# Router's 1/rms taken ahead of the last token rows, the first expert's tokens split ahead of the slot table, and the feed-forward block's first weights loaded and split ahead of the last down product

## The chip, the core and the metric

The program runs on one core of a Trainium2 chip. The metric is the device time of one execution in microseconds (us). The core has a matrix engine (PE, with its weight loads shown apart as PEld), a vector engine (DVE), a scalar engine (ACT), GpSimd (POOL) and the sync engine (SP), which issues most of the loads. Each engine runs its own list of instructions in order. An instruction that waits for a semaphore holds up everything behind it in that list, and 16 DMA engines move the data.

## The reference

Two transformer blocks stand one behind the other, over 512 tokens of 1024 features, in float32. The first ends in a mixture of experts (MoE), the second begins with a feed-forward block (FFN). Cut to what the change touches:

```python
# end of the first block: h = rms_norm(x, norm_ffn_g), then two of 32 experts for each token
g_sel = argmax(h @ w_rg + b_rg)                     # one of 4 groups
top_v, top_i = top_k(expert logits of that group, 2)
e_w = softmax(top_v) * g_w
x = x + sum over the two experts of
        e_w * ((silu(h @ w_gate[e]) * (h @ w_up[e])) @ w_down[e])
x = rms_norm(x, norm_final_g)
# second block
x = x + 0.5 * ((silu(n @ w1_gate) * (n @ w1_up)) @ w1_down)   # n = rmsnorm(x, g_ffn1), 2816 wide
...                                                 # attention, then a second FFN
```

Every token's weight for an expert and the list of the tokens of each expert hang on the router's result, so they are known only at run time.

## The kernel before

The activations x lie in SBUF with features on the partitions, as 8 blocks of 128 features by 512 tokens. A float32 product is made of three passes on PE (`mm3`, lines 257 to 259). Both operands are split first into a rounded part and its remainder (`hilo`, lines 203 and 204): a cast on ACT gives `wh` (or the first half of a `t8`), and a subtraction on DVE gives `wl` (or its second half). Weights come in 1 MB tiles (`t8`, loaded on SP at line 238). Each tile gives two or four pairs of `wh` and `wl`, from a pool `wp` of three buffers each, so a fourth split waits until PE has done with the first pair.

**The router.** While the last projection of the mixer runs, each finished block k of x is squared and added to `hsq` (L215 on ACT, L217 on DVE), multiplied with the router's weights (L573), scaled (L576), transposed to rows (L579) and copied (L581). The rows are written to DRAM as `hrow` (L673). Then 1/rms is made from `hsq`: eight small products with ones on PE (L286), `var` (L315), a square root on ACT (L268) and a few small DVE operations give `rtok` (L273). From the logits DVE finds both experts of each token. Experts are ranked by their number of tokens. Two fixed experts come first; they have tables of their own (`tabf`), and their tokens are gathered by POOL with an indirect DMA from `hrow` (L1042). For the other 30 DVE works out a slot for each token and choice (L785 to L795; `dest`, cast to integers at L794). POOL scatters the pairs to a table in DRAM in eight indirect DMAs (L804) and loads it back as `tabb` for large experts and `tab2` and `tab3` for small ones (L824, L827, L832). The gathers of the third and later units read from these.

**The experts.** The units stand in a fixed order (`SEQ`): two fixed experts, a pair of small ones, a large one, and so on. The loop in `moe` takes turns: `up` of unit n+1 is issued ahead of `down` of unit n, and the features of unit n+2 (`expert_x`, L1052, or `small_x`, L954) between them. So PE transposes the gathered tokens of unit 2 right behind `up` of unit 1 and ahead of `down` of unit 0. `expert_x` splits the tokens with `hilo`. Weight loads go up to 13 tiles ahead (`MOE_WINDOW`); an expert's number is loaded to SP's registers first (L634). Large experts split their weights with two splits ahead of use (`SPLITS`). Small ones use the loaded tile as it is.

**The end of the MoE.** The last unit's up product (L972) is followed by its down product (L1005, scaled by L1011 and L1012). `spill` then holds a loop for experts with more tokens than a table holds (L896). Its body runs zero times with these inputs, but each engine goes through its branches and a barrier there. Behind it the last unit's result is added to x, block by block (L1024 on PE, L1025 on DVE), and each block is split for the FFN (L208 on ACT, L209 on DVE), whose first product is `w1_gate`'s.

The order on each engine is chosen by a scheduler when the kernel is built, from the program order and the dependences. Instructions given to `keep_in_program_order` are not moved against what stands around them. The functions below call these.

Of the kernel before, what the change touches and what calls it, by code (L numbers as in the profile page):

```python
# [117 lines left out]
class Net:  # L118
    def __init__(self, tc, ctx, A, out):
        self.tc, self.nc, self.A, self.out, self.ctx = tc, tc.nc, A, out, ctx  # L120
        nc = self.nc
        ec = ctx.enter_context
        self.own = None
        self.const = ec(tc.tile_pool(name="const", bufs=1))
        self.p8 = ec(tc.tile_pool(name="p8", bufs=16))
        self.p4 = ec(tc.tile_pool(name="p4", bufs=4))
        self.p2 = ec(tc.tile_pool(name="p2", bufs=5))
        self.wp = ec(tc.tile_pool(name="wp", bufs=3))
        self.sm = ec(tc.tile_pool(name="sm", bufs=2))
        self.pp = ec(tc.tile_pool(name="pp", bufs=8, space=PSUM))  # L130
        self.dr = ec(tc.tile_pool(name="dr", bufs=1, space=DRAM))
        c = self.const
        self.x = c.tile([128, ND, T], F32, name="x")
        self.vec = c.tile([128, NV], F32, name="vec")
        nc.scalar.dma_start(self.vec, A["vec"])
        self.cc = c.tile([128, NC_], F32, name="cc")
        nc.scalar.dma_start(self.cc, A["cc"])
        self.ident = self.cc[:, C_ID:C_ID + 128]
        self.ones = c.tile([128, 128], F32, name="ones")
        nc.vector.memset(self.ones, 1.0)  # L140
        self.table = self.dr.tile([ROUNDS * 128 * NE, 4], I32, name="table")
        self.ordd = self.dr.tile([1, NE], I32, name="ordd")
        self.hrow = self.dr.tile([T, D], F32, name="hrow")
        self.pay = c.tile([128, NT, 2, 4], I32, name="pay")
        self.br = c.tile([128, NG + NE], F32, name="br")
        self.order = c.tile([128, NE], I32, name="order")
        self.payf = c.tile([128, NT, NFIXED, 4], F32, name="payf")
        self.payi = c.tile([128, NT, 2], F32R, name="payi")
        self.g12 = c.tile([128, ND], F32, name="g12")
        o1, o2 = VOFF["norm_final_g"], VOFF["g_ffn1_2"]  # L150
        nc.vector.tensor_tensor(self.g12, self.vec[:, o1:o1 + ND], self.vec[:, o2:o2 + ND], op=ALU.mult)
# [48 lines left out]

    def hilo(self, hi, lo, src):
        nc = self.nc
        nc.scalar.copy(hi, src)  # L203
        nc.vector.tensor_tensor(lo, src, hi.bitcast(F32), op=ALU.subtract)  # L204

    def half(self, hi, lo, src, g):

# [346 lines left out]
    def router(self):  # L554
# [14 lines left out]

        def step(k):  # L570
            self.square(acc, self.x[:, k, :], k == 0)
            for i in range(NT):
                nc.tensor.matmul(lg[:, i * W:i * W + W], self.x[:, k, i * 128:i * 128 + 128], wr[:, k, :],  # L573
                                 start=k == 0 and i == 0, stop=k == ND - 1, skip_group_check=True)
# [53 lines left out]
    def mload(self, n):  # L628
        while self.wat < min(n, len(self.wkeys)):
            nm, p, h = self.wkeys[self.wat]  # L630
            if p not in self.wreg:
                e = p
                if p >= NFIXED:
# [1 line left out]
                self.wreg[p] = self.moe_weights(e)  # L635
            self.wraw[nm, p, h] = self.load8(self.wreg[p]["gud".index(nm)][h])()
            self.wat += 1

    def raw_next(self, key):

# [20 lines left out]
    def moe(self):  # L661
# [5 lines left out]
        ur, er = two[:, 0:128], two[:, 128:256]  # L667
        nc.gpsimd.tensor_copy(ur, self.cc[:, C_U:C_U + 128])
        nc.gpsimd.tensor_copy(er, self.ones)
        rt = self.rstd([self.hsq], D, "rtok")  # L670
        hrow, table, pay, payf = self.hrow, self.table, self.pay, self.payf
        for i in range(NT):
            nc.scalar.dma_start(hrow[i * 128:i * 128 + 128, :], rows[i])  # L673
# [101 lines left out]
        nc.vector.tensor_tensor(pf[0], o1[:, :, fx], bc(ds, NFIXED), op=mul)  # L775
        nc.vector.tensor_tensor(pf[0], pf[0], pf[1], op=add)
        nc.vector.tensor_copy(pf[1], rt.rearrange("p (i o) -> p i o", o=1).to_broadcast([128, NT, NFIXED]))
        for e in range(NFIXED):
            fixed2(e)
        P = small("P", NE)  # L780
        rowr, row, tmp = P, Em, P

        def all4(t):
            return t.rearrange("p (o e) -> p o e", o=1).to_broadcast([128, NT, NE])
        nc.vector.tensor_tensor(rowr, rk3, all4(less), op=add)  # L785
        nc.vector.scalar_tensor_tensor(rowr, rowr, 127.5, all4(less), op0=ALU.is_ge, op1=mul)
        nc.vector.tensor_tensor(rowr, rowr, rk3, op=add)
        nc.vector.scalar_tensor_tensor(row, rowr, float(NE), all4(rank), op0=mul, op1=add)
# [53 lines left out]
            else:  # L842
                self.gather(self.xts[n % 2][0:CAP], tabs[p][0:CAP])

        def features(n):
            xt = self.xts[n % 2]
            return self.expert_x(xt) if SEQ[n][0] < NBIG else self.small_x(xt)

        def up(n, xT, ys=()):
            unit = SEQ[n]  # L850
            tab = tabs[unit[0]]
# [12 lines left out]
        def down(n, aT):  # L864
# [3 lines left out]
            y = self.expert_down(self.split_next, aT, tab) if unit[0] < NBIG else self.small_down(unit, aT, tab)  # L868
            self.presplit(self.wnext + SPLITS)
            return [(t, sel) for t in y]  # L870
        a, ys = up(0, features(0)), ()
        xT = features(1)
        for n in range(NU - 2):
            aT = turn(n, a)
# [4 lines left out]
        aT, before = turn(NU - 2, a), ys  # L879
        ys = down(NU - 2, aT)  # L880
        a = up(NU - 1, xT, before)
        self.fst = self.ffn_stream(A["w1_gate"], A["w1_up"], A["w1_down"])
        for key in self.down_keys(SEQ[-1]):
            self.raw_next(key)
        self.add_small(ys)
        aT = turn(NU - 1, a)
        self.fst.load(FFN_FIRST)
        self.last = down(NU - 1, aT)
        self.fst.split(1)
        self.spill(rounds, trow)  # L890

    def spill(self, rounds, trow):
# [3 lines left out]
        with tc.For_i(1, nr, 1) as b:  # L896
            with tc.For_i(0, NE, 1) as p:
                A, B, C = (self.t8([128, 2048], dt) for dt in (F32R, F32, F32))
                P, Q = self.t2(), self.t2()
                G = self.t4([128, 1024], F32R)  # L900
                U, V = ([self.wp.tile([128, 2, 512], F32R, name=nm, tag=nm) for nm in ("wh", "wl")] for _ in range(2))
                X, Z = self.ps(), self.ps()
                self.own = {"t8": [A, B, C, B, C, B, C], "t4": [G, A[:, 0:D], A[:, D:2 * D]], "t2": [P, Q, G[:, 0:512]],
                            "w": [U, V] * 6, "ps": [X, Z, X, Z, X, X, Z] + [X, Z] * 4}
# [804 lines left out]
```

## Time and profile before

| what | value |
|---|---|
| time, median of 3 runs | 2027.65 us (2027.0 to 2028.92) |
| the profiled execution's own time | 2028.41 us |
| its span (first to last instruction) | 2026.5 us, so 1.9 us lie around it |
| busy share of the span | PE 95%, DVE 64%, ACT 35%, POOL 2% |
| mean granted clock of PE | 0.978 of full speed |
| read from memory | 339 MB, 170 GB/s over the span |

Times in the rows are microseconds from the start of the span. PE's busy share hides that the stretch from about 545 to 945 us, most of the MoE, has its DMA engines busy all the time, which the other stages don't.

### The profile page before, as it was taken

To read this page: it belongs to the slowest core of one execution; us is meant where nothing else is said; L and a number is where in the kernel's file an instruction comes from. 1 tells how busy PE (TensorE), PEld (TensorE's weight loads), DVE (VectorE), ACT (ScalarE), POOL (GpSimd) and SP (SyncE) were. 2 spreads that over 40 slices of the span, in tenths; PEclk is the share of its full clock that TensorE was granted. 3 is DMA by queue.
4 is the path that set the end of the run, shared out by engine and by line. 5 is a ranking of instruction groups with operands and counts; after the bars stand their busy time and mean duration, and the time that the engine had idled before them with its cause. 6 is when DMAs were issued, how large, how long until landed. Compare 5 with 4: busy or idle time off the path is not lost.

```text
span 2026.5 us, 24440 instructions
## 1 busy us (share of the span) xinstructions
PE 1918.1 (95%) x9375; PEld 1428.8 (71%) x9375; DVE 1293.8 (64%) x2234; ACT 715.6 (35%) x1116; POOL 48.4 (2%) x69
## 2 busy tenths in 40 slices
PE   7999999979998899887999999999989999999997
PEld 5898888867554353332788888887867788888886
DVE  7999997457777575555754442459999755444323
ACT  5334325345343221111532322336366633223221
POOL 0000001003000000000000000000000000000000
PEclk9999999988999999999999999999999999999998
DMA  6121232527999999998232224130111122222311
GB/s 258 53 87 60 104 124 104 236 108 271 385 409 409 408 416 408 410 420 334 85 104 94 94 79 170 66 151 1 53 50 47 48 83 92 96 94 83 151 57 42
DMA packets 60087, 341.59 MB, mean 169 GB/s; under 512 B 8208, under 2 KB 9168, under 8 KB 27456
## 3 DMA queue, kind: packets, MB, share of 16 engines
q1 hardware_dynamic: 55152, 329.87, 42.2%
q0 software_dynamic: 3520, 6.35, 1.0%
q10 hardware_dynamic: 1296, 3.79, 0.5%
q8 instruction: 74, 1.21, 0.2%
q14 instruction: 45, 0.37, 0.1%
HBM read 339.37 MB, written 4.54 MB: 170 GB/s over the span
## 4 chain that ended last, share of the span: by engine, by line
PE 47%; DVE 3%; ACT 2%; issue 0%; DMA 0%; DVEq 0%; ACTq 0%; SPq 0%
PE ps L257 15%; PE ps L259 14%; PE ps L258 14%; PE ps L1550 1%; ACT t L1524 1%; PE ps L1537 1%; DVE wl L204 0%; DVE t L204 0%; PE ps L1292 0%; ACT wh L203 0%; PE ps L1555 0%; DVE t L1520 0%; ACT t L203 0%; PE ps L295 0%; PE ps L1293 0%
## 5 line engine op out<-in xcount | busy, mean ns | idle before, releaser
L257 PE MATMUL ps<-t,wl 128*128 128x512 f32 x1728 | 684.2, 397 | 18.7 <-ACT t L208 18.3
L258 PE MATMUL ps<-t,wh 128*128 128x512 f32 x1728 | 681.2, 394 | 0.9 <-DVE t L209 0.9
L259 PE MATMUL ps<-t,wh 128*128 128x512 f32 x1728 | 681.4, 394 | 0.0
L203 ACT CAST wh<-t 128x1024 fp32r<-128x1024 f32 (+3 forms) x321 | 324.9, 1017 | 716.9 <-PE ps L259 532.7
L204 DVE TENSOR_TENSOR wl<-t,wh 128x1024 fp32r<-128x1024 f32 (+3 forms) x321 | 378.3, 1183 | 212.0 <-ACT wh L203 208.8
L257 PEld LDWEIGHTS ps<-t,wl 128*128 128x128 f32 x1728 | 325.3, 188 | 96.9 <-ACT t L208 19.1
L258 PEld LDWEIGHTS ps<-t,wh 128*128 128x128 f32 x1728 | 326.0, 189 | 76.8 <-DVE t L209 2.3
L259 PEld LDWEIGHTS ps<-t,wh 128*128 128x128 f32 x1728 | 325.3, 188 | 75.4
L257 PE MATMUL ps<-wh,t 128*128 128x256 f32 (+2 forms) x440 | 147.4, 337 | 23.2 <-DVE t L204 23.2
L972 PE MATMUL ps<-t,t 128*32 128x512 f32 (+1 forms) x832 | 162.6, 606 | 5.5 <-DMA t<-in_w_up 3.6
L403 DVE SCALAR_TENSOR_TENSOR t<-t,vec,t 128x512 f32<-128x512 f32 x240 | 165.7, 745 | 0.4
L1025 DVE TENSOR_TENSOR x<-x,ps 128x512 f32<-128x512 f32 x200 | 126.4, 683 | 44.9 <-PE ps L1024 44.1
L258 PE MATMUL ps<-wl,t 128*128 128x256 f32 (+2 forms) x440 | 145.7, 331 | 0.0
L259 PE MATMUL ps<-wh,t 128*128 128x256 f32 (+2 forms) x440 | 144.4, 328 | 0.0
L257 PEld LDWEIGHTS ps<-wh,t 128*128 128x128 f32 x440 | 85.8, 195 | 33.0 <-DVE t L204 25.1
L972 PEld LDWEIGHTS ps<-t,t 128*32 128x32 f32 (+1 forms) x832 | 41.4, 123 | 91.7 <-issue 78.8
L1181 DVE TENSOR_TENSOR t<-ps,rbc 128x512 f32<-128x512 f32 x44 | 30.4, 690 | 115.6 <-PE ps L259 115.6
L259 PEld LDWEIGHTS ps<-wh,t 128*128 128x128 f32 x440 | 85.9, 195 | 7.4
L258 PEld LDWEIGHTS ps<-wl,t 128*128 128x128 f32 x440 | 86.0, 195 | 6.8
L1024 PEld LDWEIGHTS ps<-t,t 128*128 128x128 f32 x248 | 42.8, 190 | 67.1 <-issue 31.6
L1024 PE MATMUL ps<-t,t 128*128 128x512 f32 x248 | 78.7, 424 | 11.5 <-DVE t L1012 7.4
L203 ACT CAST t<-t 128x512 fp32r<-128x512 f32 (+2 forms) x102 | 62.7, 619 | 57.5 <-DVE t L1182 26.2
(317 smaller groups left out, 1597.1 us busy)
## 6 DMA issues: line engine op xcount, KB each, us to landing
t<-in_w_down SPq DMA_DIRECT2D x80, 1024.0 KB, 19.8
t<-in_w_gate SPq DMA_DIRECT2D x64, 1024.0 KB
t<-in_w_up SPq DMA_DIRECT2D x64, 1024.0 KB, 19.2
t<-in_w_in SPq DMA_DIRECT2D x24, 1024.0 KB, 4.7
t<-in_w_gate SPq DMA_DIRECT2D x44, 512.0 KB
t<-in_w_up SPq DMA_DIRECT2D x44, 512.0 KB, 3.4
t<-in_w_down SPq DMA_DIRECT2D x8, 768.0 KB, 11.4
t<-in_w_qi SPq DMA_DIRECT2D x4, 1040.0 KB, 4.7
```

The source lines that it names most:

```text
L203: nc.scalar.copy(hi, src)
L204: nc.vector.tensor_tensor(lo, src, hi.bitcast(F32), op=ALU.subtract)
L257: mm(acc, a[1], b[0], start=first, stop=False)
L258: mm(acc, a[0], b[1], start=False, stop=False)
L259: mm(acc, a[0], b[0], start=False, stop=last)
L403: nc.vector.scalar_tensor_tensor(y[c], src, w, y[c], op0=mul, op1=add)
L972: nc.tensor.matmul(p[o:o + c, :], xT[:, k * CAP + i:k * CAP + i + c], w[:, q, :], start=k == 0, stop=k == ND - 1)
L1024: self.nc.tensor.matmul(p, yT[:, k * 128:k * 128 + 128], sel, start=j == 0, stop=j == n - 1)
L1025: self.nc.vector.tensor_tensor(self.x[:, k, :], self.x[:, k, :], p, op=ALU.add)
L1181: nc.vector.tensor_tensor(a, accs[1], rbc, op=mul)
L1524: nc.scalar.activation(part(i), part(i), AF.Exp, bias=nm[:, i:i + 1], scale=scale, accum_out=su[:, i:i + 1])
L1537: nc.tensor.transpose(tb[b][:, o + (i - s) * 128:o + (i - s) * 128 + 128], P[:, self.PO[i] + s * 128:self.PO[i] + s * 128 + 128], self.ident)
```

## The change

Four things are done.

1. The 1/rms (`rstd`) is built in the router's last step, ahead of the last block's transposes and of the writes of `hrow`.
2. In `moe`, the first weight splits and the features of unit 0 are issued ahead of the slot table. `keep_in_program_order` holds the splits and the first operation of the slot table (`rowr`) in their places.
3. At the end of the MoE the first two pieces of the FFN's weights (`w1_gate` and `w1_up`, 0.5 MB each) are loaded into one `t8` tile by a new `ffn_first`, called just ahead of the last unit's four down loads, and are split (`self.fst.split(FFN_FIRST)`, with `FFN_FIRST = 2`) ahead of its down product. Before, they were loaded behind the down loads, and one was split behind the down product, the other behind the loop.
4. The loop body in `spill` takes two of its working tiles from `t8` in place of `wp`. It is not executed with these inputs.

```diff
     def hilo(self, hi, lo, src):
         nc = self.nc
-        nc.scalar.copy(hi, src)
-        nc.vector.tensor_tensor(lo, src, hi.bitcast(F32), op=ALU.subtract)
+        pin = self.pin or (lambda ins: ins)
+        pin(nc.scalar.copy(hi, src))
+        pin(nc.vector.tensor_tensor(lo, src, hi.bitcast(F32), op=ALU.subtract))
...
             self.square(acc, self.x[:, k, :], k == 0)
+            if k == ND - 1:
+                self.rt = self.rstd([acc], D, "rtok")
             for i in range(NT):
...
             nm, p, h = self.wkeys[self.wat]
+            if (nm, p, h) == ("d", SEQ[-1][0], 0):
+                self.ffn_first()
...
+    def ffn_first(self):
+
+        A = self.A
+        self.fst = self.ffn_stream(A["w1_gate"], A["w1_up"], A["w1_down"])
+        t = self.t8([128, FFN_FIRST, ND, 128])
+        for i in range(FFN_FIRST):
+            self.nc.sync.dma_start(t[:, i], A[("w1_gate", "w1_up")[i % 2]][i // 2])
+            self.fst.raw[self.fst.items[i][0]] = t[:, i]
+        self.fst.load(FFN_FIRST)
...
-        rt = self.rstd([self.hsq], D, "rtok")
+        rt = self.rt
...
+        self.pin = tc.keep_in_program_order
+        self.presplit(SPLITS)
+        self.pin = None
         for e in range(NFIXED):
             fixed2(e)
+
+        def features(n):
+            xt = self.xts[n % 2]
+            return self.expert_x(xt) if SEQ[n][0] < NBIG else self.small_x(xt)
+
+        xT = features(0)
...
-        nc.vector.tensor_tensor(rowr, rk3, all4(less), op=add)
+        tc.keep_in_program_order(
+            nc.vector.tensor_tensor(rowr, rk3, all4(less), op=add))
...
-        a, ys = up(0, features(0)), ()
+        a, ys = up(0, xT), ()
...
         a = up(NU - 1, xT, before)
-        self.fst = self.ffn_stream(A["w1_gate"], A["w1_up"], A["w1_down"])
         for key in self.down_keys(SEQ[-1]):
             self.raw_next(key)
+        self.fst.split(FFN_FIRST)
         self.add_small(ys)
         aT = turn(NU - 1, a)
-        self.fst.load(FFN_FIRST)
         self.last = down(NU - 1, aT)
-        self.fst.split(1)
         self.spill(rounds, trow)
...
-                U, V = ([self.wp.tile([128, 2, 512], F32R, name=nm, tag=nm) for nm in ("wh", "wl")] for _ in range(2))
+                U, V = ([w[:, j] for j in range(2)] for w in (self.t8([128, 2, 2, 512], F32R) for _ in range(2)))
```

In the changed kernel the same statements have higher line numbers (`hilo` L205 and L206, `dest` L820, the scatters L830, the gathers L1062, `wl` and `t8` as before).

**DVE, the slot table and the first splits.** Before, the list reads as follows from the last reductions of the slot table on. `t8_3626` is the first expert's tokens, and `wl_3669` the fourth weight split; the first three stand further up, between the mixer's last blocks.

```order
L693 TENSOR_REDUCE rr0_3565<-t2_3444 128x4
L815 TENSOR_REDUCE cm_3600<-ce_3601 128x1
L794 CAST dest_3563<-rr0_3565 128x4
L792 TENSOR_TENSOR t2_3444<-t2_3444 128x128
...
L204 TENSOR_TENSOR t8_3626<-ps_3627,t8_3626 128x512
L794 CAST dest_3563<-rr1_3569 128x4
L818 TENSOR_SCALAR cm_3600<-cm_3600 128x1
L204 TENSOR_TENSOR t8_3626<-ps_3634,t8_3626 128x512
...
L204 TENSOR_TENSOR wl_3669<-t8_3011,wh_3668 128x1024
L204 TENSOR_TENSOR wl_3685<-t8_3013,wh_3684 128x1024
```

In the changed kernel the same stretch reads as follows; `wl_3663` is the third split, and the tokens are `t8_3567`.

```order
L206 TENSOR_TENSOR wl_3663<-t8_3009,wh_3662 128x1024
L206 TENSOR_TENSOR t8_3567<-ps_3568,t8_3567 128x512
L206 TENSOR_TENSOR t8_3567<-ps_3575,t8_3567 128x512
L811 TENSOR_TENSOR t2_3444<-ps_3481,less_3528 128x128
...
L709 TENSOR_REDUCE rr0_3588<-t2_3444 128x4
L841 TENSOR_REDUCE cm_3623<-ce_3624 128x1
L206 TENSOR_TENSOR wl_3669<-t8_3011,wh_3668 128x1024
L820 CAST dest_3586<-rr0_3588 128x4
...
L206 TENSOR_TENSOR wl_3685<-t8_3013,wh_3684 128x1024
L820 CAST dest_3586<-rr1_3592 128x4
```

The tokens' split moved ahead of the slot table. The fourth and the fifth weight split moved ahead of the first and the second cast to `dest`.

**POOL, the gathers of units 2 and 3.** Before, behind the table's loads, the gather of unit 2 (a pair of small experts, by `tab3`) stands ahead of that of unit 3 (a large one, by `tabb`).

```order
L832 DMA tab3_3620<-table_85 32x56
L832 DMA tab3_3620<-table_85 32x52
L832 DMA tab3_3620<-table_85 32x56
L832 DMA tab3_3620<-table_85 32x52
L1042 DMA t8_2990<-hrow_87,tab3_3620 64x1024
L1042 DMA t8_2990<-hrow_87,tabb_3615 128x1024
```

In the changed kernel:

```order
L858 DMA tab3_3643<-table_85 32x56
L858 DMA tab3_3643<-table_85 32x52
L858 DMA tab3_3643<-table_85 32x56
L858 DMA tab3_3643<-table_85 32x52
L1062 DMA t8_2990<-hrow_87,tabb_3638 128x1024
L1062 DMA t8_2990<-hrow_87,tab3_3643 64x1024
```

The two gathers changed places.

**DVE at the loop of `spill`.** Before, one of the last unit's two scalings (L1012) and one weight split of the FFN stand ahead of the loop's branches (L896), and these rows behind them:

```order
L896 COMPARE_AND_BRANCH
L896 UNCONDITIONAL_BRANCH
L1012 SCALAR_TENSOR_TENSOR t4_7290<-ps_7273,tab3_3620,t4_7290 64x512
L204 TENSOR_TENSOR wl_7529<-t4_7262,wh_7528 128x1024
L1025 TENSOR_TENSOR x_78<-x_78,ps_7554 128x512
L204 TENSOR_TENSOR wl_7543<-t4_7536,wh_7542 128x1024
L209 SCALAR_TENSOR_TENSOR t8_7534<-x_78,g12_93,t8_7532 128x512
```

In the changed kernel two weight splits and neither scaling stand ahead of the branches, and these rows behind them:

```order
L916 COMPARE_AND_BRANCH
L916 UNCONDITIONAL_BRANCH
L1032 SCALAR_TENSOR_TENSOR t4_7297<-ps_7280,tab3_3643,t4_7297 64x512
L1045 TENSOR_TENSOR x_78<-x_78,ps_7551 128x512
L1032 SCALAR_TENSOR_TENSOR t4_7297<-ps_7280,tab3_3643,t4_7297 64x512
L211 SCALAR_TENSOR_TENSOR t8_7531<-x_78,g12_93,t8_7529 128x512
```

The two `wl` splits are gone from between the scaling and the first split block of x, and both scalings now stand behind the branches.

## Rows read from the trace of the kernel before

**Rows 1.** Windows: us, busy (instructions) of PE, PEld, DVE, ACT, POOL, PEclk, DMA share, GB/s.

```profile
516.00:520.00 4.00, 4.00 (x19) 3.23 (x18) 2.11 (x3) 2.60 (x3) 0.55 (x1) 1.00 1.00 417
526.00:530.00 4.00, 4.00 (x11) 3.11 (x10) 2.07 (x6) 1.05 (x1) 0.00 (x0) 0.50 1.01 420
535.00:540.00 5.00, 5.00 (x24) 4.07 (x23) 4.86 (x7) 1.71 (x2) 0.00 (x0) 1.00 0.63 239
545.00:940.00 395.00, 358.77 (x1806) 159.34 (x1798) 254.31 (x456) 87.15 (x112) 16.92 (x18) 0.97 1.01 411
950.00:952.50 2.50, 2.50 (x24) 0.66 (x16) 0.17 (x1) 0.00 (x0) 0.00 (x0) 1.00 0.25 102
```

**Rows 2.** Timeline of SP: two down loads, issued just ahead of 540.

```profile
537.89 1.70 SPq L238 DMA_DIRECT2D t<-in_w_down  x2
```

**Rows 3.** Timeline of PE, last down product to the FFN's first product.

```profile
948.86 4.10 PE L1005 MATMUL ps<-t,t 128*32 128x512 f32 x32 [0.52 <-DVE t L988]
956.46 0.50 PE L1024 MATMUL ps<-t,t 128*128 128x512 f32 x1 [3.49 <-DVEq L896]
961.58 1.22 PE L257 MATMUL ps<-t,wl 128*128 128x512 f32 x2 [4.62 <-ACT t L208]
```

**Rows 4.** Timeline of PE: start, us, engine, line, operation, [idle before <-releaser].

```profile
443.38 1.07 PE L286 MATMUL ps<-ones,t 128*128 128x2 f32 x5
...
467.00 0.79 PE L257 MATMUL ps<-wh,t 128*128 128x512 f32 x1 [1.87 <-DVE t L204]
```

**Rows 5.** Timeline of DVE, end of the mixer to the fifth weight split.

```profile
441.84 0.69 DVE L217 TENSOR_TENSOR t<-t,t 128x512 f32<-128x512 f32 x1 [0.31 <-ACT t L215]
...
465.59 0.17 DVE L794 CAST dest<-rr 128x4 int32<-128x4 f32 x1
...
466.26 0.68 DVE L204 TENSOR_TENSOR t<-ps,t 128x512 fp32r<-128x512 f32 x1
...
471.04 1.23 DVE L204 TENSOR_TENSOR wl<-t,wh 128x1024 fp32r<-128x1024 f32 x1 [2.73 <-ACT wh L203]
473.60 1.22 DVE L204 TENSOR_TENSOR wl<-t,wh 128x1024 fp32r<-128x1024 f32 x1 [1.33 <-issue]
```

**Rows 6.** Timeline of ACT, the first tokens' cast and the fourth weight cast.

```profile
464.31 0.59 ACT L203 CAST t<-ps 128x512 fp32r<-128x512 f32 x1 [12.46 <-PE ps L1052]
...
469.96 1.05 ACT L203 CAST wh<-t 128x1024 fp32r<-128x1024 f32 x1 [4.21 <-PE ps L259]
```

**Rows 7.** Timeline of POOL: first scatter, gathers of units 2 and 3.

```profile
466.06 1.05 POOL L804 DMA_INDIRECT table<-pay,dest  x1 [5.16 <-DVE t L792]
467.42 1.01 POOL L804 DMA_INDIRECT table<-pay,dest  x1 [0.30 <-issue]
...
486.94 1.00 POOL L1042 DMA_INDIRECT t<-hrow,tab  x1 [4.41 <-DMA tab<-table]
488.24 1.06 POOL L1042 DMA_INDIRECT t<-hrow,tabb  x1 [0.31 <-issue]
```

**Rows 8.** Line 1042's gathers from 455 to 560, issue to landing.

```profile
DMA to landing us min/median/max: 6.6/7.4/8.2
```

**Rows 9.** Timeline of PE: unit 2's transposes, and a stall further on.

```profile
495.57 0.71 PE L954 MATMUL ps<-cc,t 64*128 64x64 f32 x8
...
525.04 0.80 PE L257 MATMUL ps<-wh,t 128*128 128x512 f32 x1 [3.82 <-DVE t L204]
```

**Rows 10.** Timeline of ACT in the same stretch.

```profile
953.07 0.68 ACT L1011 ACTIVATE t<-ps,tab 64x512 fp32r<-64x512 f32 x1 [6.03 <-PEq L896]
...
960.81 0.72 ACT L208 ACTIVATE t<-x,g 128x512 fp32r<-128x512 f32 x1
```

**Rows 11.** Timeline of DVE in the same stretch.

```profile
954.72 1.23 DVE L204 TENSOR_TENSOR wl<-t,wh 128x1024 fp32r<-128x1024 f32 x1 [0.19 <-ACT wh L203]
958.01 0.76 DVE L1012 SCALAR_TENSOR_TENSOR t<-ps,tab,t 64x512 fp32r<-64x512 f32 x1 [2.07 <-ACT wh L203]
...
960.06 0.69 DVE L1025 TENSOR_TENSOR x<-x,ps 128x512 f32<-128x512 f32 x1
```

More of the change, by code (lines that the diff above doesn't have):

```diff
@@ L777, in moe @@
         nc.vector.tensor_copy(pf[1], rt.rearrange("p (i o) -> p i o", o=1).to_broadcast([128, NT, NFIXED]))
+        self.pin = tc.keep_in_program_order
+        self.presplit(SPLITS)
+        self.pin = None
         for e in range(NFIXED):
             fixed2(e)
+        def features(n):
+            xt = self.xts[n % 2]
+            return self.expert_x(xt) if SEQ[n][0] < NBIG else self.small_x(xt)
+        xT = features(0)
         P = small("P", NE)
@@ L843, in gather @@
                 self.gather(self.xts[n % 2][0:CAP], tabs[p][0:CAP])
-        def features(n):
-            xt = self.xts[n % 2]
-            return self.expert_x(xt) if SEQ[n][0] < NBIG else self.small_x(xt)
         def up(n, xT, ys=()):
```

## The prediction

> **What bounds the kernel now.** I read the page's slices first, then PE's waits, then the timelines of the engines around the three places that the diff touches, then windows. The span is not bound by one engine. In the router PE waits for small operations on DVE and ACT, so time saved there is saved on the clock. From about 545 to 940 the DMA engines are busy all the time, at 411 GB/s [rows 1]: what counts there is when the stream of weight loads last ran dry, and how many bytes come behind. It ran partly dry between 535 and 540, with a DMA share of 0.63 [rows 1], because SP had to wait for tile buffers that PE and DVE free, and it was fed again by the loads of 537.89 [rows 2]. At the end of the MoE PE waits again, 3.49 and 4.62 us around the loop's branches [rows 3]. From there on the change does nothing new.
>
> **The router: a gain.** DVE finishes the sum of squares at 441.84 + 0.69 = 442.53, but PE's products with ones start at 443.38, because the last transposes stand ahead of them [rows 4, 5]. Put first, they start at about 442.6, so the chain that follows (1/rms, logits, both experts, ranks, the fixed experts' gathers) is 0.8 us earlier. The transposes and the rows of `hrow` come some 1.7 us later, which the ten microseconds or more up to the first gather hide. The first tokens' cast on ACT ends at 464.31 + 0.59 = 464.90 [rows 6], yet DVE splits them only at 466.26, held by the slot table, and PE starts 0.06 us behind the split, at 467.00 [rows 4, 5]. With the table behind them the split can start at 464.9 - 0.8 = 464.1, and PE at 464.1 + 0.68 + 0.06, about 464.9: **2.1 us earlier**. The three weight splits that stood in the mixer's tail now stand here. ACT casts them in the 12.46 us that it idles [rows 6]; on DVE they take 3 x 1.23 [rows 5] among waits for PE. If the third still runs at 464.1, the gain falls to 0.9, which is the lower bound.
>
> **The slot table: a loss.** The first cast to `dest` now stands behind the fourth weight split, since the `wl` subtraction comes ahead of it in DVE's list. That split needs a buffer that PE frees only after its first matmuls: ACT's fourth cast came at 469.96, 2.96 us after PE's start, and DVE's part ended at 471.04 + 1.23 = 472.27, 5.27 after it [rows 4 to 6]. With PE's start at 464.9 it ends at 470.2. The cast to `dest`, at 465.59 before, follows it: **4.6 us later**. The second cast waits for the fifth split, which ended at 473.60 + 1.22 and now at about 472.7. The scatters that need only the first cast run first, 1.36 us apart [rows 7]; by order's list four of them come first, so the second cast is in time. Everything behind moves by 4.6: the first scatter from 466.06 to 470.7, the gather of unit 2 from 486.94 to 491.5 [rows 7].
>
> Who waits for that gather? PE, at unit 2's transposes, which stand ahead of the down product of unit 0. Before, the gather had landed by 486.94 + 6.6 = 493.5, the shortest landing of this line [rows 8], and PE came at 495.57 without a wait [rows 9]: 2.0 us to spare. Now it lands at 498.1 by that row, or at 491.5 + 8.2 = 499.7 by the longest one, since unit 3's gather, with twice the rows, goes ahead of it. I take 499.0. PE comes 2.1 us earlier, at 493.5, and stalls for 5.5. It leaves **3.4 us later** than before.
>
> As an aside, the Trainium skill (DMA: Bandwidth & Descriptors, section Anatomy of one DMA) fits an unloaded GpSimd transfer with 2.0 us plus its bytes at 436 GB/s, 2.6 us by estimate for unit 2's 256 KB. By that the gather would land at 494.1, PE would hardly stall, and the sum below would come to about -3.3. The rows' 6.6 to 8.2 beside saturated weight loads speak against it here.
>
> The stall has a second price. Behind the 3.82 us stall before 525.04 the granted clock was 0.50, the 1.2 GHz level: 11 matmuls in 4 us, where 19 run at 1.00 [rows 1, 9]. That is 1.7 us lost in each 4. A stall of 5.5 is longer; I take 5 to 6 us at the low level, so **2.4 us**, with 0 and 3 as bounds. The down product of unit 0 thus ends some 5.8 us later than before.
>
> **Is it carried to the end?** SP's loads of 537.89 wait for buffers which PE and DVE free, so they move with PE, by 5.8. The stream from there on holds the same bytes and has no gap to close, with a DMA share of 1.01 up to 940 [rows 1]. Its end moves by the same: **+5.8**. Loads that are already free to go could make up part of it. The lower bound is 3, where the clock stays up and a further microsecond is absorbed; the upper is 8, with the gather at 500 and the full clock price.
>
> **The end of the MoE.** The FFN's two pieces, 1 MB together, now go ahead of the last four down loads: at 411 GB/s [rows 1], 2.5 us more ahead of the last one. Bytes still move until about 952.5 [rows 1], and the FFN's came last, so the last down piece was in by about 950.0. The second half of the down product (32 matmuls in 4.10 from 948.86) needs it at 950.9 [rows 3]: 0.9 to spare, so that the product ends **1.6 us later** (bounds 0 and 2.5).
>
> Behind it, PE's first FFN product came at 961.58, 8.6 us after the down product's end at 952.96 [rows 3]. In that time DVE did one split ahead of the branches until 954.72 + 1.23 = 955.95 and another between the scaling (958.01 + 0.76) and the addition to x at 960.06 [rows 11]. Both, and their casts, now lie ahead of the down product, in time in which ACT waited 6.03 us [rows 10] and DVE waited for PE. Worked forward, in offsets from the end of the down product: ACT's first scaling ends at 0.8 (953.75). PE passed the branches 0.5 after DVE arrived (956.46 against 955.95); I allow 1.5, since DVE resumed only 2.1 after it [rows 3, 11], so DVE's scaling runs from 2.3 to 3.1, the product with the one-hot to 3.7, the addition (0.69) to 4.4, ACT's L208 (0.72 [rows 10]) to 5.2. That is 8.6 - 5.2 = **3.4 us gained** (2.8 to 4 with the barrier's price). Both scalings now stand behind the branches, which this counts. Net of the 1.6, the end gains 1.8.
>
> **The sum** is +5.8 - 1.8 = +4.0 us: 2032.4 against the profiled execution's 2028.41. That execution lies 0.8 above the median of 2027.65, so for a median I predict 2031.6. A difference under 0.2%, 4.1 us, is about what a measurement of this kernel can't tell from none: the forecast lies at its edge.
>
> **Rivals.**
> - *Faster: the late gather costs nothing that lasts.* The place is PE at unit 2's transposes. It decides if the gather lands within 2.0 us of its issue, or if the 3.4 and the clock's price are absorbed by loads that go early. What stays is -2.1 - 1.8, about -3.9 (2023.8), and -5.5 (2022.2) if the FFN's bytes delay nothing. For it speaks that the share of 0.63 leaves 1.85 us that an earlier load could fill; against it, that no gather of this line landed under 6.6, and that loads wait for PE.
> - *No change that shows: a shorter stall.* The gather lands at 498.1, PE's clock stays up, and the carried part is 2 to 3: the sum is 0 to +1.5 (2027.7 to 2029.2). For it speaks that the clock's price is read from one other stall.
> - *A larger loss: a wait in place of the split at the loop.* The barrier is met by an engine other than ACT or DVE, so that the end gains little, while the FFN's bytes hold the last down product for the full 2.5. With +5.8 this is +7 to +9 (2034.7 to 2036.7). For it speaks that ACT and DVE did not resume together; against it, that the engine which arrived last was DVE, with the split that goes.
>
> **Chances.** Forecast (+2 to +6) 0.45, faster rival 0.22, no change 0.20, larger loss 0.13. The forecast's range lies on both sides of 4.1, so about 0.28 of it counts as slower and 0.17 as the same: slower 0.41, same 0.37, faster 0.22. The likeliest case alone spans 2029.6 to 2033.6. The range reaches to 2023.4, which takes in most of the faster rival, and to 2035.8.
>
> **What would show it.** In the changed profile: the products with ones at 442.6, PE's first expert matmul near 464.9, the first cast to `dest` right behind a `wl` subtraction near 470, a PE wait of about 5 us at unit 2's transposes near 494 with the clock at 0.50 behind it, the gap in the DMA share near 541 to 546, the last down product ending some 7 us later than 952.96, and 5 us from there to the first FFN matmul. If PE does not wait at unit 2's transposes, the prediction's largest term is wrong. If it waits and the MoE's end does not move with it, the carrying is.

## The result, and the profile after

The changed kernel is slower by 0.6%. In the runs behind the prediction its median was 2041.85 us against 2028.92 (ratio 1.0056, 95% interval 1.0045 to 1.0067), and in the five rounds of the first experiment 2042.99 against 2030.21 (1.0062, 1.0049 to 1.0075): 11 to 13 us, where +4.0 was forecast and 2035.8 was the range's upper end. One execution of the changed kernel took 3816.1 us with a 128x512 matmul at 677 ns on average instead of 397, and its profile was drawn from that one, so the rows of after come from a profiled execution of the first experiment, which took 2037.70 us (span 2035.8). That is the shortest of its five, 9.3 us over the profiled execution of before.

The forecast's first steps show. On PE (timeline: start, us, line, [idle before <-releaser]) the products with ones, L288 now, start at 442.38 instead of 443.38, the first expert's product at 464.05 instead of 467.00, and then there is the wait at unit 2's transposes (L974), of 11.80 us, where before shows none [rows 4, 9]:

```profile
464.05 0.79 PE L259 MATMUL ps<-wh,t 128*128 128x512 f32 x1 [0.55 <-DVE t L206]
...
503.98 1.11 PE L974 MATMUL ps<-cc,t 64*128 64x64 f32 x8 [11.80 <-DMA t<-hrow,tab]
```

DVE's timeline has the first tokens' split at 463.31, later the fourth `wl`, and directly behind it the first cast to `dest`, 3.65 us later than before [rows 5]:

```profile
468.10 1.23 DVE L206 TENSOR_TENSOR wl<-t,wh 128x1024 fp32r<-128x1024 f32 x1 [1.33 <-ACT wh L205]
469.24 0.16 DVE L820 CAST dest<-rr 128x4 int32<-128x4 f32 x1
```

On POOL the first scatter follows at 469.69. The first load of the table waits 4.80 us for the scatters to land, and unit 2's gather (`tab`) is issued at 493.01, 6.1 us later than before [rows 7], and lands 10.97 us after that, when PE goes on:

```profile
469.69 1.06 POOL L830 DMA_INDIRECT table<-pay,dest  x1 [9.71 <-DVE t L818]
...
485.62 0.59 POOL L850 DMA_DIRECT2D tabb<-table  x1 [4.80 <-DMA table<-pay,dest]
...
491.45 1.26 POOL L1062 DMA_INDIRECT t<-hrow,tabb  x1 [2.16 <-PE ps L261]
493.01 0.99 POOL L1062 DMA_INDIRECT t<-hrow,tab  x1 [0.30 <-issue]
```

The same wait on POOL in the kernel before, a row that stands in no group above:

```profile
478.87 0.59 POOL L824 DMA_DIRECT2D tabb<-table  x1 [1.42 <-DMA table<-pay,dest]
```

The windows of after (columns as in [rows 1]) show what follows: PE's clock is at 0.50 from 500 to 510, the stream of weights falls to a share of 0.11 from 505 to 510 and to 0.40 from 545 to 550, and is full from there to 945.

```profile
500.00:505.00 5.00, 1.02 (x8) 0.92 (x8) 0.00 (x0) 0.00 (x0) 0.00 (x0) 0.50 0.72 243
505.00:510.00 5.00, 5.00 (x13) 3.92 (x13) 2.96 (x5) 1.04 (x1) 0.95 (x1) 0.50 0.11 27
...
545.00:550.00 5.00, 5.00 (x24) 4.05 (x23) 4.85 (x6) 2.10 (x2) 0.00 (x0) 1.00 0.40 120
550.00:945.00 395.00, 361.76 (x1809) 162.89 (x1807) 254.76 (x457) 89.95 (x115) 18.68 (x19) 0.97 1.01 409
```

The loads of 537.89 [rows 2] come at 548.34 on SP:

```profile
548.34 1.71 SPq L240 DMA_DIRECT2D t<-in_w_down  x2
```

At the end of the MoE, PE's timeline has the last piece of the last up product (L992), the last unit's down product (L1025) in two pieces and the FFN's first product (L259), to be held against [rows 3]:

```profile
952.36 3.62 PE L992 MATMUL ps<-t,t 128*32 128x512 f32 x26 [1.45 <-DMA t<-in_w_up]
...
959.60 4.62 PE L1025 MATMUL ps<-t,t 128*32 128x512 f32 x20 [1.54 <-DVE tokf L1051]
965.09 1.91 PE L1025 MATMUL ps<-t,t 128*32 128x512 f32 x12 [0.87 <-SPq L916]
...
971.18 1.22 PE L259 MATMUL ps<-t,wl 128*128 128x512 f32 x2 [1.53 <-ACT t L210]
```

The end of the down product moved from 952.96 to 967.00, by 14.0; the FFN's first product from 961.58 to 971.18, by 9.6. All of that 9.6 was there at the end of the last up product (946.26 before, 955.98 now). Before, that product's last piece was:

```profile
941.13 5.13 PE L972 MATMUL ps<-t,t 128*32 128x512 f32 x26 [1.44 <-DMA t<-in_w_up]
```

### The profile page after: what moved, and what is told of

The parts are those of the page before. It is cut to its first block, busy times and chain, and to the rows that moved or that the text cites. A ratio compares the mean times of both kernels' runs of the same rounds, so it can differ in the third digit from the quotient of the medians.

```text
span 3814.2 us, 24441 instructions
## 1 busy us (share of the span) xinstructions
PE 3748.3 (98%) x9375; PEld 2277.2 (60%) x9375; DVE 1307.1 (34%) x2234; ACT 720.9 (19%) x1116; POOL 49.2 (1%) x69
## 4 chain that ended last, share of the span: by engine, by line
PE 98%; DVE 1%; issue 0%; ACT 0%; DMA 0%; DVEq 0%; ACTq 0%
PE ps L259 25%; PE ps L261 25%; PE ps L260 25%; PE ps L992 8%; PE ps L1025 4%; PE ps L1044 3%; PE ps L1570 1%; PE ps L1557 1%; PE ps L1312 1%; PE ps L1313 1%; PE ps L974 1%; PE ps L288 0%; PE ps L297 0%; PE ps L1575 0%; PE ps L451 0%
## 5 line engine op out<-in xcount | busy, mean ns | idle before, releaser
L259 PE MATMUL ps<-t,wl 128*128 128x512 f32 x1728 | 1169.1, 677 | 15.2 <-ACT t L210 15.2
L260 PE MATMUL ps<-t,wh 128*128 128x512 f32 x1728 | 1165.1, 674 | 1.2 <-DVE t L211 1.2
L261 PE MATMUL ps<-t,wh 128*128 128x512 f32 x1728 | 1165.3, 674 | 0.0
L259 PEld LDWEIGHTS ps<-t,wl 128*128 128x128 f32 x1728 | 515.7, 299 | 305.3 <-issue 267.0
L261 PEld LDWEIGHTS ps<-t,wh 128*128 128x128 f32 x1728 | 514.9, 298 | 290.6 <-issue 270.1
L260 PEld LDWEIGHTS ps<-t,wh 128*128 128x128 f32 x1728 | 514.4, 298 | 289.6 <-issue 266.0
L205 ACT CAST wh<-t 128x1024 fp32r<-128x1024 f32 (+3 forms) x321 | 324.4, 1014 | 1810.7 <-PE ps L261 1418.2
L206 DVE TENSOR_TENSOR wl<-t,wh 128x1024 fp32r<-128x1024 f32 (+3 forms) x321 | 379.2, 1183 | 730.9 <-ACT wh L205 730.5
L992 PE MATMUL ps<-t,t 128*32 128x512 f32 (+1 forms) x832 | 323.7, 1138 | 0.0
L259 PE MATMUL ps<-wh,t 128*128 128x256 f32 (+2 forms) x440 | 229.0, 522 | 20.0 <-DVE t L206 20.0
L260 PE MATMUL ps<-wl,t 128*128 128x256 f32 (+2 forms) x440 | 230.3, 523 | 0.0
L261 PE MATMUL ps<-wh,t 128*128 128x256 f32 (+2 forms) x440 | 230.1, 523 | 0.0
L259 PEld LDWEIGHTS ps<-wh,t 128*128 128x128 f32 x440 | 143.6, 326 | 46.8 <-DVE t L206 22.9
L992 PEld LDWEIGHTS ps<-t,t 128*32 128x32 f32 (+1 forms) x832 | 55.8, 159 | 192.0 <-issue 190.6
L261 PEld LDWEIGHTS ps<-wh,t 128*128 128x128 f32 x440 | 145.5, 331 | 25.6 <-issue 24.3
L1025 PE MATMUL ps<-t,t 128*32 128x512 f32 (+1 forms) x416 | 156.5, 1132 | 1.4 <-DVE tokf L1051 1.4
L260 PEld LDWEIGHTS ps<-wl,t 128*128 128x128 f32 x440 | 143.2, 325 | 24.0 <-issue 20.0
L1044 PE MATMUL ps<-t,t 128*128 128x512 f32 x248 | 128.7, 681 | 2.2 <-DVE t L1032 2.2
```

The source lines that it names most:

```text
L205: pin(nc.scalar.copy(hi, src))
L206: pin(nc.vector.tensor_tensor(lo, src, hi.bitcast(F32), op=ALU.subtract))
L259: mm(acc, a[1], b[0], start=first, stop=False)
L260: mm(acc, a[0], b[1], start=False, stop=False)
L261: mm(acc, a[0], b[0], start=False, stop=last)
L992: nc.tensor.matmul(p[o:o + c, :], xT[:, k * CAP + i:k * CAP + i + c], w[:, q, :], start=k == 0, stop=k == ND - 1)
```

## The experiments

The theory at this point: the late gather makes PE wait and the stream of weights run dry, and that is the whole loss. The rival: the end of the MoE costs much of it.

**The changed kernel again** (no edit).

> The changed kernel as it is, for a profile with PE at its usual speed. Late-gather theory (mine): PE waits some 5 us at unit 2's transposes near 494, with the clock at 0.50 behind it; the last down product ends 7 us or more later than 952.96; the time is 10 to 13 us above before. Rival, the end of the MoE: the wait at unit 2's transposes is under 2 us, and most of the loss lies behind 920, around the last down product and the loop's branches.

Ratio 1.0062 (1.0049 to 1.0075); its rows are those above. The wait is there, over twice as long as expected, and the loss lies ahead of 920.

**The router's and the slot table's part alone.** The edit takes `ffn_first` out again.

```diff
-            if (nm, p, h) == ("d", SEQ[-1][0], 0):
-                self.ffn_first()
...
+        self.fst = self.ffn_stream(A["w1_gate"], A["w1_up"], A["w1_down"])
         for key in self.down_keys(SEQ[-1]):
             self.raw_next(key)
-        self.fst.split(FFN_FIRST)
         self.add_small(ys)
         aT = turn(NU - 1, a)
+        self.fst.load(FFN_FIRST)
         self.last = down(NU - 1, aT)
+        self.fst.split(1)
```

> The router's and the slot table's part alone (1/rms early, splits and tokens ahead of the table); the end of the MoE as before. Late-gather theory: this part loses, +6 us by my sum and +10 to +13 if it carries the whole loss. Rival, the end of the MoE: -2 to +1 us here.

2041.38 us, ratio 1.0051 (1.0038 to 1.0064), about 10 us: by the times this part carries the loss. Its profiled execution doesn't show how: at 2034.25 us it was the shortest of five by 3 us. PE came to the transposes 5.3 us later than in the changed kernel (it had stood 2.85 us at 481.95 for something that the profile doesn't name, and its clock was 0.59 from 484 to 490), unit 2's gather landed in 5.4 us, and so the wait was short. The longer four were not profiled.

```profile
497.68 0.71 PE L964 MATMUL ps<-cc,t 64*128 64x64 f32 x8 [0.16 <-DMA t<-hrow,tab]
```

**The end of the MoE alone.** The kernel before with `ffn_first`, the two early splits and the two tiles of `spill`, by the same lines of the change.

```diff
+            if (nm, p, h) == ("d", SEQ[-1][0], 0):
+                self.ffn_first()
...
+        self.fst.split(FFN_FIRST)
         self.add_small(ys)
         aT = turn(NU - 1, a)
-        self.fst.load(FFN_FIRST)
         self.last = down(NU - 1, aT)
-        self.fst.split(1)
```

> The end of the MoE alone (FFN's first weights loaded ahead of the last down loads and split ahead of the down product); the router as before. Late-gather theory: -2 us (1.6 lost on the later down load, 3.4 won at the loop), so a ratio of 0.999. Rival, the end of the MoE: +5 us or more, a ratio of 1.0025 or above.

2029.76 us, ratio 0.9994 (0.9985 to 1.0003): -1.2 us, with no change inside the interval. The rival falls. The profile gives one thing more. Here the slot table is as before, and yet PE waits 0.74 for unit 2's gather, which was issued at 487.53 and so landed 8.83 us later (first POOL, then PE):

```profile
487.53 1.62 POOL L1052 DMA_INDIRECT t<-hrow,tab  x1 [4.69 <-PE ps L259]
...
496.36 0.68 PE L964 MATMUL ps<-cc,t 64*128 64x64 f32 x8 [0.74 <-DMA t<-hrow,tab]
```

In the kernel before, PE came 8.63 us after the issue [rows 7, 9], and in its profile this very gather (the view of L1042 from 486 to 488) landed after 6.6. So the 2.0 us to spare of the prediction were there in that execution, but not in this one:

```profile
DMA to landing us min/median/max: 6.6/6.6/6.6
```

At the end of the MoE, the down product starts 1.54 us behind the transposes instead of 0.52 [rows 3], since a weight split stands ahead of the copy that it needs on DVE. It then runs at a clock of 0.57 (950 to 954), and its second piece waits 1.03:

```profile
950.25 4.47 PE L1015 MATMUL ps<-t,t 128*32 128x512 f32 x20 [1.54 <-DVE tokf L1041]
955.74 1.91 PE L1015 MATMUL ps<-t,t 128*32 128x512 f32 x12 [1.03 <-SPq L906]
```

From the end of the up product to that of the down product it is 11.0 us (946.63 to 957.65), against 6.7 before; from there to the FFN's first product 4.2, against 8.6.

**Both casts to `dest` ahead of the later splits.** The whole change, with the third and later splits pinned behind them.

```diff
-            nc.vector.tensor_copy(dest[:, :, j:j + 1], rr)
+            tc.keep_in_program_order(nc.vector.tensor_copy(dest[:, :, j:j + 1], rr))
...
+        self.pin = tc.keep_in_program_order
         a, ys = up(0, xT), ()
+        self.pin = None
```

> The whole change, but with the third and later weight splits held behind both casts to the slot numbers, so that the scatters start near 466 again and the tokens' split still comes early. Late-gather theory: unit 2's gather lands by 494, PE waits under 1 us at unit 2's transposes, and the time falls to 2 to 4 us under before. Rival, the end of the MoE: within 2 us of the changed kernel.

2037.55 us, ratio 1.0039 (1.0026 to 1.0053): some 5 us less than the changed kernel, 8 over before. Neither expectation holds, and the first scatter went out at 469.16, not near 466. In this execution PE started the first expert 2.0 us later than in the changed kernel's profile, so the places are better compared from that start: the first cast stood 1.4 us ahead of it before [rows 4, 5], stood 5.2 behind it in the changed kernel, and stands 2.65 behind it here (first PE, then DVE). The fourth split in its way is thus 2.5 of the 6.6 us. The other 4.1 come from what this edit keeps, the first tokens and the first splits ahead of the slot table (with the slot table first, below, the cast stands 1.4 ahead again).

```profile
466.05 0.79 PE L259 MATMUL ps<-wh,t 128*128 128x512 f32 x1 [0.55 <-DVE t L206]
```

```profile
468.70 0.17 DVE L820 CAST dest<-rr 128x4 int32<-128x4 f32 x1
```

The scatters' landing is the other thing that I had missed: the table's first load still waits 5.26 us for it, and PE 7.66 for the gather.

```profile
487.08 0.59 POOL L850 DMA_DIRECT2D tabb<-table  x1 [5.26 <-DMA table<-pay,dest]
...
503.29 1.11 PE L976 MATMUL ps<-cc,t 64*128 64x64 f32 x8 [7.66 <-DMA t<-hrow,tab]
```

So there were two new questions: what makes the scatters land late, and what the exchange of the gathers costs.

**Unit 2's gather first again.** An order is imposed on the gathers of units 2 and 3 on POOL.

```diff
-                self.gather(self.xts[n % 2][0:CAP], tabs[p][0:CAP])
+                ins = self.gather(self.xts[n % 2][0:CAP], tabs[p][0:CAP])
+            if n == 3:
+                tc.add_manual_dep(ins.ins, self.gathered.ins.name, mybir.DependencyInfo(
+                    mybir.DependencyClass.NoSync, mybir.DependencyReason.DATA), reason="in order")
+            self.gathered = ins
```

> The changed kernel with one thing put back: unit 2's gather goes ahead of unit 3's again. If unit 3's 512 KB in front is what made unit 2's gather land 10.9 us after its issue, it lands within 8 us now, PE's wait at unit 2's transposes falls from 11.8 us to 6 to 9, and the time by 3 to 5 us. Rival, weight loads on the same DMA engines slow every small transfer: the landing stays at 9 us or more and the time within 2 us of the changed kernel.

2039.27 us, ratio 1.0045 (1.0031 to 1.0058). The landing fell from 10.97 to 8.35 us and PE's wait to 9.53; the time is some 3 us lower, but the intervals of the two ratios overlap, so a gain in time is not shown.

```profile
501.85 1.11 PE L978 MATMUL ps<-cc,t 64*128 64x64 f32 x8 [9.53 <-DMA t<-hrow,tab]
```

**Both of these.** The edits of the last two experiments together.

> The changed kernel with both casts to the slot numbers ahead of the third weight split and unit 2's gather ahead of unit 3's. Late-gather theory: PE waits 2 to 5 us at unit 2's transposes, and the time lies 2 to 4 us over before. Rival, weight loads slow every small transfer: the scatters' last landing and the gather stay slow, PE waits 6 us or more, 5 to 8 us over before.

2040.62 us, ratio 1.0044 (1.0030 to 1.0057). PE waits 8.13: the rival's side, with a time above even its range, and no better than the casts' edit alone. The wait for the scatters is 4.89 here too. The gather took 9.17 us with unit 2's ahead again, against 7.94 in the run with the casts' edit alone, where unit 3's went 3.5 us ahead of it. The two pairs of runs disagree, so what the exchange costs is not settled.

**The slot table first.** The kernel before with the early 1/rms (the hunks here) and the new end of the MoE (the diff of that experiment), without the first tokens' early split.

```diff
+            if k == ND - 1:
+                self.rt = self.rstd([acc], D, "rtok")
...
-        rt = self.rstd([self.hsq], D, "rtok")
+        rt = self.rt
...
```

> The slot table put back ahead of the splits and the first tokens, with the early 1/rms and the new end of the MoE kept. Late-gather theory: no wait over 1 us at unit 2's transposes, and the time 1 to 3 us under before (0.8 from the early products with ones, the rest from the end of the MoE). Rival, the early 1/rms or the split's move out of the mixer's tail is what loses: 5 us or more over before.

2027.59 us, ratio 0.9987 (0.9978 to 0.9996): 2.6 us under before, faster than both kernels. The table's first load waits 1.43, and PE comes to the transposes without a wait:

```profile
478.51 0.59 POOL L838 DMA_DIRECT2D tabb<-table  x1 [1.43 <-DMA table<-pay,dest]
...
495.41 0.71 PE L966 MATMUL ps<-cc,t 64*128 64x64 f32 x8
```

**A second profile of the changed kernel** (no edit).

> The changed kernel once more, for a second profile, since its times spread from 2037.7 to 2043.9. Late-gather theory: an execution that is longer by some us has the same amount more at unit 2's transposes. Rival, the spread comes from elsewhere: the wait there stays at 11 to 12 us.

2039.94 us, 2.2 more than the first profile's execution, with a wait of 12.82, 1.0 more. The other 1.2 us had arisen ahead of the wait: PE came to the transposes that much later, after a first expert's product at 465.44 instead of 464.05. So neither expectation is the whole of it: executions differ ahead of the wait too.

```profile
506.22 1.12 PE L974 MATMUL ps<-cc,t 64*128 64x64 f32 x8 [12.82 <-DMA t<-hrow,tab]
```

**Weight loads held behind the scatters.** In the changed kernel SP's load of 475.93 waits for the last scatter.

```diff
+            if self.wat in (16, 17):
+                tc.add_manual_dep(self.loaded.ins, self.scattered.ins.name, mybir.DependencyInfo(
+                    mybir.DependencyClass.Sync, mybir.DependencyReason.DATA), reason="behind the scatters")
```

> The changed kernel, with the weight load that SP issued at 475.93, and all loads behind it, held until the last scatter has landed. If weight loads on the same DMA engines slow the scatters, POOL's wait ahead of the first table load falls from 4.8 us to under 2.5, and unit 2's gather is issued 2 us or more earlier. Rival, the wait belongs to the scatters themselves: it stays above 4 us. The time may move either way, since unit 1's weights come later.

POOL's wait falls to 1.42 us, exactly that of the kernel before, with a DMA share of 0.02 while the scatters land, from 482.35 to 483.80. Unit 2's gather goes out at 492.78, and, measured from the first expert's product (465.67 here), 1.9 us earlier than in the changed kernel. The time is 2036.24 us, ratio 1.0029 (1.0019 to 1.0039), about half of the loss gone. The gather itself still takes 8.97 us, beside loads that now run with a share of 1.01 (496 to 502).

```profile
483.77 0.59 POOL L856 DMA_DIRECT2D tabb<-table  x1 [1.42 <-DMA table<-pay,dest]
...
501.75 1.11 PE L980 MATMUL ps<-cc,t 64*128 64x64 f32 x8 [8.02 <-DMA t<-hrow,tab]
```

```profile
482.35:483.80 1.45, 1.45 (x7) 1.21 (x7) 1.45 (x2) 1.00 (x2) 0.03 (x2) 1.00 0.02 1
```

The first fence is POOL and PE, the second windows. In the changed kernel the scatters land from 480.80 to 485.60, with a share of 0.85; before, from 477.40 to 478.90, with 0.02:

```profile
480.80:485.60 4.80, 4.80 (x22) 3.90 (x22) 4.20 (x5) 3.41 (x5) 0.02 (x1) 1.00 0.85 312
```

```profile
477.40:478.90 1.50, 1.50 (x8) 1.23 (x7) 1.35 (x2) 1.18 (x2) 0.08 (x2) 1.00 0.02 1
```

**Down product of unit 0 ahead of unit 2's transposes.**

```diff
-            xT = features(n + 2)
+            if n:
+                xT = features(n + 2)
             ys = down(n, aT)
+            if not n:
+                xT = features(n + 2)
```

> The changed kernel with unit 2's transposes issued behind unit 0's down product instead of ahead of it. Late-gather theory: PE does the 6 us of the down product before it waits, its wait at the transposes falls from 11.8 us to about 6, and the time by 4 to 6 us, to 5 to 8 over before. Rival, the time is set by the table's loads and the stream of weights behind it, whatever PE does meanwhile: within 2 us of the changed kernel.

2036.39 us, ratio 1.0028 (1.0016 to 1.0039): 6 to 7 us under the changed kernel. PE's wait is 4.73, since it has the down product to do first. So about half of the loss hangs on PE's place in its list.

```profile
504.32 1.11 PE L977 MATMUL ps<-cc,t 64*128 64x64 f32 x8 [4.73 <-DMA t<-hrow,tab]
```

**The FFN's splits behind the copy.** The kernel with the slot table first, with both splits pinned behind the last unit's `turn`.

```diff
-        self.fst.split(FFN_FIRST)
         self.add_small(ys)
         aT = turn(NU - 1, a)
+        self.pin = tc.keep_in_program_order
+        self.fst.split(FFN_FIRST)
+        self.pin = None
         self.last = down(NU - 1, aT)
```

> The kernel with the slot table first, with the FFN's two splits held behind the last unit's copy for its down product. If the split ahead of that copy and the clock behind the longer wait are what lengthened the last down product (10 us from the end of the up product in place of 6.7), its start comes 1 us earlier, it runs at full clock, and the time falls by 1 to 3 us. Rival, the later down loads alone lengthen it: within 1 us of the kernel with the slot table first.

2028.57 us, ratio 0.9990 (0.9981 to 0.9998), the same as without it. The down product starts 0.52 behind the transposes again and gains nothing: it meets two waits inside instead, and 16 matmuls take 3.98 us. So the later loads are what is left, though the profile names SP's branch as the releaser of these waits, not a DMA.

```profile
948.76 1.05 PE L1021 MATMUL ps<-t,t 128*32 128x512 f32 x4 [0.52 <-DVE t L1004]
950.00 3.98 PE L1021 MATMUL ps<-t,t 128*32 128x512 f32 x16 [0.18 <-SPq L912]
955.26 1.91 PE L1021 MATMUL ps<-t,t 128*32 128x512 f32 x12 [1.28 <-SPq L912]
```

**The early 1/rms alone.** The first two hunks of the slot-table-first edit.

> The early 1/rms alone. By my sum -0.8 us, a ratio of 0.9996, from products with ones that start at 442.6 in place of 443.4. Rival, nothing of it reaches the end because the stream of weights sets it: 0 to +0.5 us. What moved the three first splits out of the mixer's tail is also in here or not, by the order that the scheduler chose.

2029.30 us, ratio 0.9994 (0.9985 to 1.0003): -1.2 us, in line with -0.8 and not to be told from none. The splits' move out of the mixer's tail is not in here. The end of the MoE is the old one, and yet the last down product's second piece waits 0.94 us, which the profile of before doesn't show:

```profile
940.04 3.62 PE L974 MATMUL ps<-t,t 128*32 128x512 f32 x26 [1.44 <-DMA t<-in_w_up]
...
949.97 1.91 PE L1007 MATMUL ps<-t,t 128*32 128x512 f32 x12 [0.94 <-SPq L898]
```

## Why the prediction was wrong

The way it would go was right, and the place: the fourth `wl` ahead of the cast to `dest`, the late table, PE's wait at unit 2's transposes, the low clock behind it, the stream's later start. The size was not. Step by step, forecast against the profiles of before and after:

| step | forecast | measured |
|---|---|---|
| products with ones | -0.8 | -1.0 |
| first expert's product | -2.1 | -2.95 |
| first cast to `dest` | +4.6 | +3.65 |
| scatters' landing ahead of the table's load | no change | 1.42 to 4.80 |
| issue of unit 2's gather | +4.6 | +6.1 |
| from its issue to landing | 7.5 | 10.97 (9.55 in the second profile) |
| PE's wait / how much later it leaves | 5.5 / +3.4 | 11.80 / +8.4 |
| low clock behind the wait | +2.4 | +2.7 (unit 0's down product ends 11.1 later) |
| end of the last up product | +5.8 | +9.7 (start of its last piece +11.2) |
| last down product's own lengthening | +1.6 | +4.3 (+2.8 from the start of that piece) |
| down product to the FFN's first product | -3.4 | -4.4 |
| sum | +4.0 | +9.6 at the FFN's first product, +9.3 over the two profiled executions, +11 to +13 in the medians |

The mechanism held. The step that failed is how much later PE leaves unit 2's transposes, put at 3.4 us and measured at 8.4, and two sizes in it were wrong. First, "Everything behind moves by 4.6" took the chain from the first scatter to the gather as one of fixed durations. The scatters came 3.6 us later, and the weight load that SP issued at 479.39 before comes at 475.93 (first before, then after), as PE starts earlier:

```profile
479.39 0.33 SPq L238 DMA_DIRECT2D t<-in_w_gate  x1
```

```profile
475.93 0.33 SPq L240 DMA_DIRECT2D t<-in_w_gate  x1
```

So the scatters moved against the loads by 7.1 us, out of a stretch with a DMA share of 0.02 into one of 0.85, and their landing cost 3.4 more; holding the loads back took exactly that away. Second, "I take 499.0" gave unit 2's gather 7.5 us, from landings of 6.6 to 8.2 before, and it took 10.97. That unit 3's gather ahead of it is the cause is not shown, as the runs with the order put back disagree. In all, the wait was 6.3 us longer than forecast, 5.0 of it later departure and 1.3 an earlier arrival of PE.

The 2.0 us to spare were no safe ground either. Unit 2's gather landed in 6.6 us in the profile of before, but in three other profiles with the old order of the slot table (the end of the MoE alone, the FFN's splits behind the copy, the early 1/rms alone) it took 8.7, 8.6 and 7.1, and PE waited 0.74, 0.37 and 0.45. That was luck of the execution that was read.

What hung on this step held. The clock's price was nearly as taken, and the delay was carried to the end (+10.4 at the loads of 537.89, +11.2 where the last up product's last piece starts). The faster rival needed a landing under 2.0 us or loads that make up for it. Neither came: unit 2's gather landed in 5.4 us at the least, in any profile of these runs, and the delay of the loads stayed.

The end of the MoE came out at about nothing (-1.2 us by the ratio, forecast -1.8), by two larger terms. The gain at the branches was 4.4, since PE's whole way from the down product to the FFN fell to 4.2. The down product's 4.3 in the table is too much for this change: before, the last piece of the up product took 5.13 us for the 26 matmuls that took 3.62 after, so that its end, but not the loads behind it, came 1.5 later. From the start of that piece, which waits for its weights, to the end of the down product it is 11.83 us before, and 11.83 and 11.84 in the two other profiles with the old end. In all ten profiles with the new end it is 14.60 to 14.64, with the split ahead of the copy or behind it, and with the first 20 matmuls in as little as 2.77 us (with the slot table first, 949.77 to 952.54). The rows of that run:

```profile
940.84 5.32 PE L984 MATMUL ps<-t,t 128*32 128x512 f32 x26 [1.45 <-DMA t<-in_w_up]
...
953.53 1.91 PE L1017 MATMUL ps<-t,t 128*32 128x512 f32 x12 [0.99 <-SPq L908]
```

So the place of the split and the clock did not count; the order of the loads cost 2.8, where the prediction had 2.5 less 0.9 to spare. The spare was not there. Net, that is -1.6, close to the -1.8 of the forecast, with both terms about 1 us too small.

By the Trainium skill (DMA: Bandwidth & Descriptors, section Queues, rings and completion order) each DMA engine takes turns between the queues that it has work for, a packet at a time. The runs agree as far as they go, since the scatters on POOL's queue landed later the more the engines were busy with SP's loads: after 1.4 to 1.7 us at a share of 0.02 to 0.08, 3.6 to 3.9 at 0.74 to 0.79, and 4.8 to 5.3 at 0.85 to 1.03. That turns by packet are the reason, no run here shows.

Open are three things: why the medians differ by up to 3 us more than the two profiles do, as no execution near 2043 was profiled, what made the executions of the first part alone longer than its profiled one, and what made the gather of the changed kernel take 10.97 us, when others took 6.6 to 9.2 at as high a DMA share.

## What to carry to other kernels

A chain of small transfers has no duration of its own: when it is moved, read the DMA share of the stretch that it moves into, take each transfer's landing from several executions beside that share, and leave the range open upward where there are none. Pulling weight splits and the next product's operands forward is paid for by whatever stands behind them on the same engine, so look for the instruction there that starts a chain of transfers, and for everything that it waits for. Here it was not enough to put the two casts ahead of the later splits (ratio 1.0039). With the whole slot table ahead, the same early 1/rms and the early FFN weights were a gain of 2.6 us (ratio 0.9987).

## What the runs showed of the hardware

The wait of POOL for its eight scatters, after it was done with the last one, grew with the DMA share of that stretch: 1.42 us at 0.02 (the kernel before, and the changed kernel with the loads held back), 1.67 at 0.08 (the end of the MoE alone), 3.56 at 0.74 (the first part alone), 4.80 at 0.85 (the changed kernel), 5.26 at 1.03 (both casts ahead).

The share alone doesn't tell the landing of a gather. One of 64 rows of 4 KB landed in 6.6 to 9.2 us at shares of 0.94 to 1.02, in 5.4 at 0.86, and in 10.97 at 0.96 and 9.55 at 0.85 with a gather of 128 rows issued 1.4 to 1.6 us ahead of it on the same queue.
